# A relative-bias table that the host spreads over queries and near keys, loaded by one plain DMA

## The chip, the cores and the metric

The kernel runs on one core of a Trainium2 chip. The metric is the device time of one execution in microseconds (us). The kernel before took 1336.9 us as the median of three runs, which lay between 1336.58 and 1338.81 us. All data is float32; most large products split their operands into two float32r parts and take three passes over them.

## The reference

One encoder layer over 1024 tokens of 1024 features. A combined input projection feeds two head groups, their outputs are concatenated and projected, and a SwiGLU network with 2816 hidden features follows. Of it, only the attention group touches the changed table:

```
score = sum_h iw[h] * relu(iq[h] . ik)          # the indexer, 4 heads
idx   = top 256 keys of each query, chunk-causal
logits = q . k[idx] / 8 + rel_bias[t5_bucket(idx - qpos)]
p = softmax(logits);  out = p @ v[idx]
```

`rel_bias` has 32 rows (buckets) and 8 columns (heads). `t5_bucket` depends on the distance between key and query alone. For all keys 128 or more positions back it gives bucket 15. A softmax doesn't change when a constant is added to a row, so the kernel uses `rel_bias[bucket] - rel_bias[15]` and adds nothing for far keys.

## The kernel before

Tokens are taken in 8 blocks of 128. Stage 1 is the input projection of blocks 0 to 3 (`in_proj(0)`), with 11 chunks of weight columns, each multiplied with four blocks; then the same for blocks 4 to 7, the output projection and the feed-forward network of the first half, and the same of the second. In the trace the products of the projections are the matmuls that write tile `d`; each chunk's weights are loaded from DRAM on SP's DMA queue into `wraw`, and split into `whi` (ScalarE) and `wlo` (VectorE).

Everything else runs as background work between these products: jobs are Python generators in threads (`w` weights, `sel` index scores and top-k, `key`, `ret` retention, `att` attention, `bias`, `root` norms; lines 38 to 40). At build time, `tick` (line 874) is called after every group of large products. It lets a job issue its next step when a rough clock says that the step's data is there (plus 0.7 us) and that VectorE and ScalarE have at most 4 us of backlog (2 us for `bias`). `charge` (line 802) advances that clock; it takes a DMA as 2 us plus its bytes at 250 GB/s. So the order of instructions on each engine is fixed when the kernel is built, and each engine executes its own list in order.

`bias_tables` (line 230) is such a job. It is queued by `tables` (line 1099) after the first chunk. It loads `rel_bias` and a one-hot table of 32 x 384 on ScalarE's DMA queue, multiplies them (TensorE, tile `t`), copies the 8 x 384 result to `f` (VectorE, tile `rl`), and then on SP's queue writes `f` 128 times over to a DRAM scratch (`skew`, 8 x 128 x 384 floats):

```
nc.sync.dma_start(scr[:].rearrange("p h c -> h p c"), f[:, None, :].to_broadcast([8, 128, 384]))
```

The next step reads the scratch back on SP's queue with a row pitch one element short, so that each of 128 queries gets its own shifted window of 256 near keys (`bias`, 128 x 8 x 256), and masks a corner with a memset. `attention` (line 681) waits, at build time, until `self.bias` is set, and its first reduction of every head reads `bias` (line 735): directly for blocks 0 and 1, and through `mb` (line 715) from block 2 on. The logits go to the PSUM tile `l`, of which there is one buffer (line 720), so the next head's logits wait until VectorE has read the last one's.

On SP's queue stand, beside the weights, the loads of `x` for the row norms of blocks 4 to 7 (`x_stats`, line 370, tile `maA`); ScalarE squares them into `waste`.

Of the kernel before, what the change touches and what calls it, by code (L numbers as in the profile page):

```python
# [6 lines left out]
F32 = mybir.dt.float32  # L7
# [4 lines left out]
OP = mybir.AluOpType  # L12
AX = mybir.AxisListType
PSUM = bass.MemoryType.PSUM
DRAM = bass.MemoryType.DRAM
# [3 lines left out]
KT = 8  # L19
H = 8  # L20
DH = 64
TOPK = 256
# [5 lines left out]
NEG = -1.0e30  # L28
BIG = 3.0e38
SUB = 2                      # steps in which one load of weights is split  # L30
WARM = 11                    # products of zeros while the first operands are on their way
VALUES, PAIRS, GATES = 4, 4, 2          # tiles of the retention between projection and use

# The rough clock (us) that places background work: latencies between engines, the power on GpSimd.
# [3 lines left out]
# Threads of background work: most backlog (us) of VectorE or ScalarE, jobs at once, time from the end of a step to the next.  # L38
# [6 lines left out]
def host_constants():  # L45
    f = np.float32
    pos = np.arange(S, dtype=np.float64)
    inv = 10000.0 ** (-np.arange(32, dtype=np.float64) / 32)
    ang = (pos.astype(f)[:, None] * inv.astype(f)[None, :]).astype(np.float64)
    cos = np.cos(ang).astype(f).reshape(NB, 128, 32).transpose(1, 0, 2)  # L50
    sin = np.sin(ang).astype(f).reshape(NB, 128, 32).transpose(1, 0, 2)
    lg = np.log1p(-(2.0 ** (-5.0 - np.arange(H, dtype=np.float64))))
    dq = np.exp((pos + 1.0)[:, None] * lg[None, :])
    dk = np.exp(-(pos + 1.0)[:, None] * lg[None, :]) * DH ** -0.5
    dec = np.concatenate([dq, dk], axis=1).astype(f).reshape(NB, 128, 16).transpose(1, 0, 2)
    rel = np.arange(384) - 255
    n = np.abs(rel)
    nf = np.maximum(n, 1).astype(f)
    large = 8 + (np.log(nf / f(8)) / f(np.log(16.0)) * f(8)).astype(np.int32)
    bucket = np.where(rel > 0, 16, 0) + np.where(n < 8, n, np.minimum(large, 15))  # L60
    bkt = np.zeros((32, 384), f)
    bkt[bucket, np.arange(384)] = 1.0
    bkt[15, :] -= 1.0
    bits = np.tile((np.uint32(1) << np.arange(32, dtype=np.uint32))[None, :], (128, 1))
    eye = np.eye(128, dtype=f)
    return {
        "cos": np.ascontiguousarray(cos), "sin": np.ascontiguousarray(sin),
        "dec": np.ascontiguousarray(dec), "bkt": bkt, "bits": bits, "eye": eye,
        "causal": np.triu(np.ones((128, 128), f)),
    }  # L70


def layouts(host):
    """x with the features of a block of tokens on the partitions, the weights of its norm alike."""
    x = host["x"].reshape(NB, 128, KT, 128)
    return {"xt": np.ascontiguousarray(x.transpose(0, 3, 2, 1)).reshape(NB, 128, KT * 128),
            "n1": np.ascontiguousarray(host["norm1_w"].reshape(KT, 128).T)}


def extent(v):  # L80
    """The first and the last column that an access touches in its partition."""
    lo = v.offset % v.ap[0][0] if v.ap[0][0] else 0
    return lo, lo + sum(abs(st) * (n - 1) for st, n in v.ap[1:]) + 1


class Engine:
    """An engine whose instructions also advance a rough clock of it, by which background work is placed."""
# [28 lines left out]
class Layer:  # L116
    def __init__(self, tc, a, out, stack):
        self.tc, self.nc, self.a, self.out = tc, Engines(self, tc.nc), a, out
        self.clock = {"tensor": 0.0}
        self.busy = {"vector": [], "scalar": [], "gpsimd": []}  # L120
        self.issued_at, self.at, self.floor, self.issued = 0.0, 0.0, 0.0, 0
        self.written, self.touched, self.rings = {}, {}, {}
        self.x = a["x"][0]
        self.w_in, self.w_out = a["w_in"][0], a["w_out"][0]
        self.w_gate, self.w_up, self.w_down = a["w_gate"][0], a["w_up"][0], a["w_down"][0]
        pool = lambda n, **k: stack.enter_context(tc.tile_pool(name=n, **k))
        self.per = pool("per", bufs=1)
        self.dr = pool("dr", bufs=1, space=DRAM)

# [1 line left out]
    def new(self, pool, shape, dt, tag, bufs):  # L131
        """A tile; what is known of the time when its buffer comes free goes into the clocks."""
        t = pool.tile(shape, dt, tag=tag, name=tag, bufs=bufs)
        ring = self.rings.setdefault(tag, [])
        ring.append(t[:].tensor.name)
        if len(ring) > bufs:
            self.written[ring[-1]] = [(0, 1 << 30, self.touched.get(ring[-1 - bufs], 0.0), "")]
        return t
# [26 lines left out]
    def first_loads(self):  # L165
        """What the first product waits for, the array kept at work until then."""
# [37 lines left out]
    def roots(self):  # L204
        """The roots of the means' counts, in the weights of the norms."""
        nc = self.nc
        nc.vector.tensor_scalar(self.kw, self.kw, DH ** 0.5, None, op0=OP.mult)
        nc.vector.tensor_scalar(self.kvw, self.kvw, 128 ** 0.5, None, op0=OP.mult)
# [21 lines left out]
    def bias_tables(self):  # L230
        nc, a = self.nc, self.a
        rb = self.sb([32, 8], tag="rb")
        nc.scalar.dma_start(rb, a["rel_bias"])
        bkt = self.sb([128, 512], tag="rl", bufs=2)[:32, :384]
        nc.scalar.dma_start(bkt, a["bkt"])
        yield
        p = self.pt(384)
        nc.tensor.matmul(p[:8], rb, bkt, start=True, stop=True)
        f = self.sb([128, 512], tag="rl", bufs=2)[:8, :384]
        nc.vector.tensor_copy(f, p[:8])  # L240
        scr = self.dr.tile([128, 8, 384], F32, name="skew")
        nc.sync.dma_start(scr[:].rearrange("p h c -> h p c"), f[:, None, :].to_broadcast([8, 128, 384]))
        yield
        self.bias = self.sb([128, H, 256], tag="bias")
        full = scr[:]
        nc.sync.dma_start(self.bias, bass.AP(tensor=full.tensor, offset=full.offset + 127,
                                             ap=[[8 * 384 - 1, 128], [384, 8], [1, 256]]))
        nc.vector.memset(self.bias[0:64, :, 192:256], NEG)

# [1 line left out]
    def rsqrt(self, out, ssum, eps, more=None):  # L251
        """(ssum + more + eps) ** -0.5; the root of a mean's count goes into the weights that follow."""
# [22 lines left out]
    def pieces(self, loads, step, n, rows):  # L275
        """The tiles of one chunk of weights and the steps that fill them."""
# [6 lines left out]
        def fill():  # L283
            late = None
            for i, parts in enumerate(loads):
# [3 lines left out]
                tag, bufs = ("sc", 2) if first and i == 3 else ("wraw", 3)  # the scores come later  # L289
# [22 lines left out]
    def split_in(self, src, slot, g):  # L312
        """The half g, whose features are on the partitions already."""
# [44 lines left out]
    def x_block(self, b):  # L358
        """A block of tokens, weighed and split; its columns' root mean square is left to the products' ends."""
# [10 lines left out]
    def x_stats(self, b):  # L370
        """The root mean square of a block of tokens, a step before the factors that come of it."""
# [242 lines left out]
    def topk(self, bs):  # L614
        """Exact TOPK-th largest of every row, built bit by bit in the order of the float keys; the next candidate
        is the last one with its next bit flipped, and the last bit flipped back if that was too much.

        A pass sums sign(x - t), that is 2 * #(x > t) + #(x == t) - n, so the largest t that passes is the
        wanted value or its predecessor; one exact count settles which."""
# [153 lines left out]
    def heads_out(self, b, hp, pa):  # L773
        """The sums of the products with both parts of V, two heads above each other; the sum itself a step later."""
# [27 lines left out]
    def charge(self, name, op, args, kw):  # L802
        """Advance the clock (us) of an engine by one instruction on its operands."""
# [39 lines left out]
    def book(self, name, start, cost):  # L843
        """The first time from start on at which an engine has room for an instruction."""
# [20 lines left out]
    def step(self, th, job):  # L865
        """One step of a job; whether it issued anything."""
# [293 lines left out]
```

## Time and profile before

| | |
|---|---|
| median of 3 runs | 1336.9 us |
| the profiled execution, span from first to last instruction | 1335.8 us |
| TensorE busy | 1296.0 us, 97% of the span |
| VectorE busy | 887.2 us, 66% |
| ScalarE busy | 722.7 us, 54% |
| mean granted TensorE clock | 0.989 of full speed |
| share of the chain that ended last: TensorE / VectorE / ScalarE / DMA | 66% / 13% / 11% / 5% |

The chain that ended last is followed back from the last instruction, at each step to what released it; its DMA share of 5% contains 3% for a single transfer, `skew<-rl`. Line 96 is the helper that issues every instruction, so instructions are known by their tiles. "d<-whi,Thi" is a product of `whi` and `Thi` into `d`. SPq and ACTq are the instructions that issue DMAs from SP and ScalarE; q1 is the DMA queue of SP and q10 that of ScalarE. The busy time of TensorE is modelled and overlaps, so the number of products started in a stretch says more of its pace than its busy time.

### The profile page before, as it was taken

To read this page: it belongs to the slowest core of one execution; us is meant where nothing else is said; L and a number is where in the kernel's file an instruction comes from. 1 tells how busy PE (TensorE), PEld (TensorE's weight loads), DVE (VectorE), ACT (ScalarE), POOL (GpSimd) and SP (SyncE) were. 2 spreads that over 40 slices of the span, in tenths; PEclk is the share of its full clock that TensorE was granted. 3 is DMA by queue.
4 is the path that set the end of the run, shared out by engine and by line. 5 is a ranking of instruction groups with operands and counts; after the bars stand their busy time and mean duration, and the time that the engine had idled before them with its cause. 6 is when DMAs were issued, how large, how long until landed. Compare 5 with 4: busy or idle time off the path is not lost.

```text
span 1335.8 us, 21094 instructions
## 1 busy us (share of the span) xinstructions
PE 1296.0 (97%) x7621; PEld 1123.2 (84%) x7621; DVE 887.2 (66%) x2535; ACT 722.7 (54%) x1706; POOL 55.4 (4%) x68
## 2 busy tenths in 40 slices
PE   8969998999999899999999999999999999999998
PEld 7859998999999787888888878889988888888886
DVE  6649998888987877887877776645644343434343
ACT  7648977556695788478559834432532222222221
POOL 1300011010020000000000000000000000000000
PEclk9979999999999999999999999999999999999999
DMA  8552214221242222222222222326143333333331
GB/s 289 111 135 73 80 35 125 68 72 41 64 130 77 76 68 81 78 64 82 82 78 76 79 80 65 93 86 198 57 127 96 90 97 90 96 92 95 93 92 68
DMA packets 159665, 122.86 MB, mean 92 GB/s; under 512 B 8104, under 2 KB 139848, under 8 KB 159560
## 3 DMA queue, kind: packets, MB, share of 16 engines
q1 hardware_dynamic: 153816, 113.77, 29.7%
q10 hardware_dynamic: 5744, 7.74, 1.7%
q8 instruction: 60, 0.98, 0.3%
q14 instruction: 45, 0.37, 0.1%
HBM read 115.71 MB, written 5.77 MB: 91 GB/s over the span
## 4 chain that ended last, share of the span: by engine, by line
PE 66%; DVE 13%; ACT 11%; DMA 5%; issue 4%; POOL 1%; SPq 0%; ACTq 0%; POOLq 0%; DVEq 0%
PE d L96 56%; PE t L96 8%; ACT junk L96 6%; DVE wlo L96 3%; DMA skew<-rl 3%; DVE L L96 2%; PE l L96 2%; ACT whi L96 2%; ACT L L96 1%; ACT Thi L96 1%; DVE maA L96 1%; DVE tc L96 1%; DVE tr L96 1%; DMA wraw<-in_w_in_dram 1%; ACT ph L96 0%
## 5 line engine op out<-in xcount | busy, mean ns | idle before, releaser
L96 ACT ACTIVATE whi<-wraw 128x512 fp32r<-128x512 f32 (+1 forms) x388 | 220.8, 617 | 253.9 <-PE d L96 178.0
L96 PE MATMUL d<-whi,Thi 128*128 128x256 f32 (+1 forms) x960 | 281.9, 294 | 4.8 <-DVE zqk L96 1.9
L96 PE MATMUL d<-Thi,whi 128*128 128x512 f32 (+1 forms) x736 | 285.8, 389 | 0.2 <-ACT Thi L96 0.2
L96 PE MATMUL d<-Tlo,whi 128*128 128x512 f32 (+1 forms) x736 | 284.9, 387 | 0.4 <-DVE Tlo L96 0.4
L96 PE MATMUL d<-Thi,wlo 128*128 128x512 f32 (+1 forms) x736 | 284.5, 387 | 0.0
L96 PE MATMUL d<-wlo,Thi 128*128 128x256 f32 (+1 forms) x960 | 272.2, 284 | 2.0 <-DVE wlo L96 2.0
L96 PE MATMUL d<-whi,Tlo 128*128 128x256 f32 (+1 forms) x960 | 272.4, 284 | 0.0
L96 DVE TENSOR_TENSOR wlo<-wraw,whi 128x512 fp32r<-128x512 f32 (+1 forms) x390 | 251.8, 675 | 7.1 <-ACT whi L96 6.6
L96 PEld LDWEIGHTS d<-whi,Thi 128*128 128x128 f32 x960 | 182.2, 190 | 10.5 <-DVE zqk L96 2.3
L96 PEld LDWEIGHTS d<-wlo,Thi 128*128 128x128 f32 x960 | 182.3, 190 | 3.6 <-DVE wlo L96 2.8
L96 PEld LDWEIGHTS d<-whi,Tlo 128*128 128x128 f32 x960 | 182.0, 190 | 0.2 <-issue 0.2
L96 ACT ACTIVATE junk<-sc,tc 128x384 bf16<-128x384 f32 (+5 forms) x186 | 163.5, 879 | 32.7 <-DVE tc L96 32.0
L96 PEld LDWEIGHTS d<-Thi,wlo 128*128 128x128 f32 x736 | 139.3, 189 | 30.4
L96 PEld LDWEIGHTS d<-Tlo,whi 128*128 128x128 f32 x736 | 139.4, 189 | 28.4 <-DVE Tlo L96 0.7
L96 PEld LDWEIGHTS d<-Thi,whi 128*128 128x128 f32 x736 | 139.1, 189 | 28.6 <-ACT Thi L96 0.7
L96 PE MATMUL d<-whi,hh 128*128 128x512 f32 x352 | 140.1, 398 | 0.1
L96 PE MATMUL d<-wlo,hh 128*128 128x512 f32 x352 | 139.1, 396 | 0.0
L96 PE MATMUL d<-whi,hl 128*128 128x512 f32 x352 | 138.7, 396 | 0.0
L96 DVE TENSOR_TENSOR th<-th,d 128x512 f32<-128x512 f32 x44 | 30.1, 684 | 99.4 <-PE d L96 99.3
L96 PEld LDWEIGHTS d<-whi,hh 128*128 128x128 f32 x352 | 66.2, 188 | 16.3 <-DVE maA L96 0.6
L96 PEld LDWEIGHTS d<-whi,hl 128*128 128x128 f32 x352 | 66.2, 188 | 16.0
L96 PEld LDWEIGHTS d<-wlo,hh 128*128 128x128 f32 x352 | 66.2, 188 | 14.8
(306 smaller groups left out, 1731.0 us busy)
## 6 DMA issues: line engine op xcount, KB each, us to landing
wraw<-in_w_gate_dram SPq DMA_DIRECT2D x88, 256.0 KB, 3.1
wraw<-in_w_up_dram SPq DMA_DIRECT2D x88, 256.0 KB, 3.6
wraw<-in_w_down_dram SPq DMA_DIRECT2D x44, 512.0 KB, 3.8
wraw<-in_w_in_dram SPq DMA_DIRECT2D x24, 512.0 KB, 3.7
wraw<-in_w_in_dram SPq DMA_DIRECT2D x32, 256.0 KB, 3.5
wraw<-in_w_out_dram SPq DMA_DIRECT2D x16, 512.0 KB, 3.6
maA<-in_x_dram SPq DMA_DIRECT2D x20, 256.0 KB, 5.0
wraw<-in_w_in_dram SPq DMA_DIRECT2D x7, 292.0 KB, 3.9
```

What stands on the lines that cost most here:

```text
L96: return f(*args, **kw)
```

## The change

The host now builds a table `near` of 128 x 8 x 256 floats: `rel_bias` at the bucket of (key - query - 128) for each query of a block, head and near key. The device loads it with one DMA on ScalarE's queue, loads row 15 of `rel_bias` to all partitions with another, and subtracts it on VectorE in two instructions of four heads each, one per step of the job. The one-hot table, the product, the copy, the DRAM scratch and both DMAs on SP's queue are gone. Nothing else changes but comments and docstrings.

```diff
+def buckets():
+    f = np.float32
+    rel = np.arange(256)[None, :] - np.arange(128)[:, None] - 128
+    ...
 def layouts(host):
     x = host["x"].reshape(NB, 128, KT, 128)
+    near = np.ascontiguousarray(host["rel_bias"][buckets()].transpose(0, 2, 1))
     ...
     def bias_tables(self):
         nc, a = self.nc, self.a
-        rb = self.sb([32, 8], tag="rb")
-        nc.scalar.dma_start(rb, a["rel_bias"])
-        bkt = self.sb([128, 512], tag="rl", bufs=2)[:32, :384]
-        nc.scalar.dma_start(bkt, a["bkt"])
-        yield
-        p = self.pt(384)
-        nc.tensor.matmul(p[:8], rb, bkt, start=True, stop=True)
-        f = self.sb([128, 512], tag="rl", bufs=2)[:8, :384]
-        nc.vector.tensor_copy(f, p[:8])
-        scr = self.dr.tile([128, 8, 384], F32, name="skew")
-        nc.sync.dma_start(scr[:].rearrange("p h c -> h p c"), f[:, None, :].to_broadcast([8, 128, 384]))
-        yield
-        self.bias = self.sb([128, H, 256], tag="bias")
-        full = scr[:]
-        nc.sync.dma_start(self.bias, bass.AP(tensor=full.tensor, offset=full.offset + 127,
-                                             ap=[[8 * 384 - 1, 128], [384, 8], [1, 256]]))
-        nc.vector.memset(self.bias[0:64, :, 192:256], NEG)
+        far = self.sb([128, 8], tag="far")
+        nc.scalar.dma_start(far, a["rel_bias"][15:16, :].to_broadcast([128, 8]))
+        bias = self.sb([128, H, 256], tag="bias")
+        nc.scalar.dma_start(bias, a["near"])
+        yield
+        for h in (0, 4):
+            nc.vector.tensor_tensor(bias[:, h:h + 4], bias[:, h:h + 4], far[:, h:h + 4, None].to_broadcast([128, 4, 256]),
+                                    op=OP.subtract)
+            if h == 4:
+                nc.vector.memset(bias[0:64, :, 192:256], NEG)
+                self.bias = bias
+            yield
```

## Rows read from the trace of the kernel before

**Rows 1.** Chain that ended last, 16 to 90 us: start us, us, what.
```profile
37.06 4.27 DMA rl<-in_bkt_dram
42.30 0.56 DVE rl L96
42.88 33.61 DMA skew<-rl
```

**Rows 2.** TensorE in order of time: start us, us, instruction [idle before <-releaser].
```profile
41.46 0.80 PE L96 MATMUL t<-rl,rb 32*8 32x384 f32 x2 [0.90 <-DMA rl<-in_bkt_dram]
...
83.57 0.47 PE L96 MATMUL l<-kkhi,qT 128*128 128x128 f32 x1 [11.74 <-DVE nm L96]
```

**Rows 3.** SP's queue in order of time, 48 to 77 us.
```profile
48.33 9.10 SPq L96 DMA_DIRECT2D maA<-in_x_dram  x2
...
76.55 0.38 SPq L96 DMA_DIRECT2D bias<-skew  x1
```

**Rows 4.** DMA issues from 44 to 76 us: KB each, us to landing.
```profile
maA<-in_x_dram SPq DMA_DIRECT2D x2, 256.0 KB, 26.8
wraw<-in_w_in_dram SPq DMA_DIRECT2D x1, 256.0 KB, 21.2
```

**Rows 5.** ScalarE and VectorE in order of time, 77 to 84 us.
```profile
77.16 0.63 ACT L96 ACTIVATE waste<-maA 128x512 bf16<-128x512 f32 x1 [9.09 <-DMA maA<-in_x_dram]
...
83.34 0.63 ACT L96 ACTIVATE whi<-wraw 128x512 fp32r<-128x512 f32 x1 [4.69 <-DMA wraw<-in_w_in_dram]
...
82.52 0.48 DVE L96 MEMSET bias<- 64x512 f32 x1 [2.67 <-DMA bias<-skew]
```

**Rows 6.** Stretches: us, busy PE PEld DVE ACT POOL (instructions), PEclk, DMA share, GB/s.
```profile
60.00:68.00 8.00, 8.00 (x71) 8.00 (x71) 1.97 (x6) 1.74 (x4) 0.00 (x0) 1.00 0.53 65
78.00:80.00 2.00, 0.00 (x0) 0.00 (x0) 0.58 (x4) 0.64 (x2) 1.03 (x2) 0.50 0.98 310
84.00:92.00 8.00, 7.84 (x36) 7.12 (x35) 6.67 (x19) 6.69 (x19) 0.00 (x0) 0.52 0.64 167
92.00:100.00 8.00, 7.74 (x60) 6.92 (x59) 7.49 (x21) 6.04 (x24) 0.00 (x0) 1.00 0.18 49
```

**Rows 7.** VectorE groups by shape: count | busy us, mean ns | idle before.
```profile
L96 DVE TENSOR_TENSOR mb<-bias,sc 128x512 f32<-128x512 f32 x24 | 16.4, 682 | 0.1
L96 DVE SCALAR_TENSOR_TENSOR sc<-rl,iw,sc 128x512 f32<-128x512 f32 x18 | 13.4, 746 | 4.8 <-ACT rl L96 4.8
```

**Rows 8.** DMA: the read of the scratch, its KB and us to landing; queues from 24 to 28 us.
```profile
bias<-skew SPq DMA_DIRECT2D x1, 1024.0 KB, 5.8
...
q10 hardware_dynamic: 426, 0.58, 49.5%
q1 hardware_dynamic: 456, 0.46, 34.5%
```

**Rows 9.** ScalarE's issues of the two table loads, in order of time.
```profile
35.88 0.34 ACTq L96 DMA_DIRECT2D rb<-in_rel_bias_dram  x1
...
37.06 0.33 ACTq L96 DMA_DIRECT2D rl<-in_bkt_dram  x1
```

**Rows 10.** Longer stretches, same columns as the other table of stretches.
```profile
44.00:52.00 8.00, 7.42 (x62) 7.12 (x61) 6.31 (x21) 6.01 (x19) 5.04 (x6) 1.00 0.46 48
...
40.00:200.00 160.00, 144.77 (x1157) 137.28 (x1156) 125.00 (x511) 115.40 (x354) 20.03 (x21) 0.95 0.34 80
100.00:200.00 100.00, 98.41 (x818) 93.79 (x817) 91.86 (x413) 82.83 (x260) 9.01 (x8) 1.00 0.22 63
340.00:400.00 60.00, 59.69 (x503) 59.15 (x502) 52.37 (x184) 47.54 (x112) 10.52 (x10) 1.00 0.34 106
...
460.00:465.00 5.00, 2.35 (x12) 1.69 (x12) 4.90 (x14) 5.00 (x16) 0.00 (x0) 0.87 0.50 141
465.00:470.00 5.00, 5.00 (x24) 4.82 (x23) 2.86 (x9) 1.11 (x3) 0.00 (x0) 0.50 0.64 174
```

**Rows 11.** VectorE in order of time: the end of block 0's attention.
```profile
108.98 0.19 DVE L96 RECIPROCAL rec<-sums 128x8 f32<-128x8 f32 x1
```

More of the change, by code (lines that the diff above doesn't have):

```diff
@@ L14 @@
 PSUM = bass.MemoryType.PSUM
-DRAM = bass.MemoryType.DRAM
 S, D = 1024, 1024
@@ L55, in host_constants @@
     dec = np.concatenate([dq, dk], axis=1).astype(f).reshape(NB, 128, 16).transpose(1, 0, 2)
[L56 to L63, printed above, removed]
     bits = np.tile((np.uint32(1) << np.arange(32, dtype=np.uint32))[None, :], (128, 1))
@@ L67, in host_constants @@
         "cos": np.ascontiguousarray(cos), "sin": np.ascontiguousarray(sin),
-        "dec": np.ascontiguousarray(dec), "bkt": bkt, "bits": bits, "eye": eye,
+        "dec": np.ascontiguousarray(dec), "bits": bits, "eye": eye,
         "causal": np.triu(np.ones((128, 128), f)),
     }
+def buckets():
+    f = np.float32
+    rel = np.arange(256)[None, :] - np.arange(128)[:, None] - 128
+    n = np.abs(rel)
+    nf = np.maximum(n, 1).astype(f)
+    large = 8 + (np.log(nf / f(8)) / f(np.log(16.0)) * f(8)).astype(np.int32)
+    return np.where(rel > 0, 16, 0) + np.where(n < 8, n, np.minimum(large, 15))
 def layouts(host):
     x = host["x"].reshape(NB, 128, KT, 128)
+    near = np.ascontiguousarray(host["rel_bias"][buckets()].transpose(0, 2, 1))
     return {"xt": np.ascontiguousarray(x.transpose(0, 3, 2, 1)).reshape(NB, 128, KT * 128),
-            "n1": np.ascontiguousarray(host["norm1_w"].reshape(KT, 128).T)}
+            "n1": np.ascontiguousarray(host["norm1_w"].reshape(KT, 128).T), "near": near}
 def extent(v):
@@ L127, in __init__ @@
         self.per = pool("per", bufs=1)
-        self.dr = pool("dr", bufs=1, space=DRAM)
     def new(self, pool, shape, dt, tag, bufs):
```

## The prediction

> **What bounds the kernel now.** The page comes first: TensorE is busy 97% of the span, so the end moves only where TensorE waits or where its clock is low. The chain of waits comes second, because it names what stands there. Its one long piece that isn't a product is the write of the DRAM scratch: 33.61 us from 42.88 us on, ahead of it the load of the one-hot table (4.27 us) and the copy of its product (0.56 us) [rows 1]. The third view is TensorE in order of time: in that stretch it stands still for 11.74 us, up to 83.57 us, at the logits of a second attention head; they need the PSUM buffer that VectorE empties, which is to read the bias [rows 2]. SP's list shows why the bias is so late: the read of the scratch could be issued only at 76.55 us, after the write had landed [rows 3], and VectorE, which executes its list in order, stood until 82.52 us at the memset that waits for that read [rows 5].
>
> The write also holds up what is behind it. Two loads for the row norms took 9.10 us to be issued [rows 3] and 26.8 us to land, a load of weights 21.2 us [rows 4]; a read of 1024 KB, four times as much as one of these, landed in 5.8 us [rows 8]. ScalarE waited for those norms until 77.16 us and for weights until 83.34 us [rows 5]. So bias, norms and weights are late together, all behind one write; with it, all three waits go. Last, the table of stretches: by 78 us the granted clock is 0.50, its lower level of 1.2 GHz, after TensorE had been idle, and from 84 to 92 us it is 0.52 while TensorE works [rows 6].
>
> **The change part by part.** The profiled execution spans 1335.8 us; the median is 1336.9, so what lies around the span and the difference between runs make 1.1 us, which I add at the end.
>
> *The stall.* Removed with the write and the read: 11.74 us of idle TensorE [rows 2]. I take all of it, 11.7. Next in line in that stretch would be the weights, but they were late only behind the write.
>
> *The clock.* Between 84 and 92 us TensorE started 36 products, between 60 and 68 us, at full clock and with nothing late, 71 [rows 6]: 8 x (1 - 36/71) = 3.9 us lost. The clock alone gives the same: 8 x (1 - 0.52) = 3.8 us. If the attention's own chain paces this stretch as it does from 92 to 100 us at full clock (60 products), the loss is 8 x (60 - 36)/71 = 2.7 us; I take 3.9, since the count and the clock agree. The 8 x (1 - 60/71) = 1.2 us of the stretch from 92 to 100 us I don't count: attention is in the queue there whatever the bias does.
>
> *The product.* TensorE waits 0.90 us for the one-hot table and works 0.80 us in two passes [rows 2]: 1.7 us gone. At least the 0.8 goes; something else that is late there could take the wait.
>
> *The new loads.* They are issued on ScalarE's queue where the old two were, at 35.9 to 37.1 us [rows 9], the big one right behind the small one, some 36.3 us. The table has as many bytes as the read of the scratch, which landed in 5.8 us [rows 8]: 42.1 us. Weights and norms are on SP's queue at the same time. From 24 to 28 us, when both queues were full, ScalarE's moved 0.58 MB, 0.145 MB/us [rows 8]; by that, 1.05 MB take 7.2 us and, with some 2 us for its start and its end (an estimate: 5.8 us less the 4.0 that 1.05 MB take at both queues' 0.26 MB/us), the table lands at 45.5. When does VectorE come to it? The old product was reached at 41.46 - 0.90 = 40.6 us, 4.7 us after its load; the rough clock had put 2.2 + 0.7 us between them. It puts 6.2 + 0.7 us between the new load and the first subtraction, 4.0 more: 44.6 us. So VectorE waits from 0 to 0.9 us, in a place where it is idle anyway (6.31 of 8 us busy from 44 to 52 us [rows 10]).
>
> Here the Trainium skill speaks against a second queue (DMA: Bandwidth & Descriptors, "Queues, rings and completion order"): each DMA engine takes turns between the queues that have work for it, so a load from ScalarE's queue takes its share from SP's. The trace agrees: both queues were served side by side from 24 to 28 us [rows 8]. By the rule the table lands at 45.5 us, by the lone transfer at 42.1; what a much later landing does is the second rival.
>
> *VectorE.* Two subtractions of 128 x 1024. A two-operand instruction on 128 x 512 takes 0.68 us, the slowest kind of that shape 0.75 [rows 7]; twice the columns give 1.36 to 1.5 us, less the fixed part, so 1.3 us each. The copy of 0.56 us [rows 1] goes, the memset stays: 2 x 1.3 - 0.56 = 2.0 us more. VectorE has 8 - 6.31 = 1.7 us free from 44 to 52 us [rows 10], which hides most: I charge 0.5; without cover it is 2.0. What stands behind the subtractions on VectorE are splits of weights and the index scores; whoever waits for those is TensorE.
>
> *What is late next.* VectorE's work doesn't go, it moves into less time. From 40 to 200 us it is busy 125.0 of 160 us [rows 10]; afterwards (125.0 + 2.0)/(160 - 17.3) = 89%, about the 92% of 100 to 200 us, where TensorE starts 818 products in 100 us against 71 in 8 [rows 6, 10]. The mix differs (attention has products of other sizes), so 1 - 8.18/8.88 = 8% is an upper bound of what a loaded VectorE costs; over the 40 us from 44 to 84 us, which had no attention so far, that is 3.2 us. The lower bound is 0. I take 2.0, nearer the upper end, since the row that it rests on is the same work.
>
> *Sum.* 1335.8 - 11.7 - 3.9 - 1.7 + 0.5 + 2.0 = 1321.0 us of span, and 1.1: **1322 us**. TensorE is the bound before and after; top-k and the attention of later blocks start earlier by the same amount, so I let the gain stand to the end.
>
> **Rivals.**
> *The new order also removes a later stall.* From 460 to 470 us TensorE idles 2.65 of 5 us and then has the clock at 0.87 and 0.50 [rows 10]: 2.65 + 0.13 x 2.35 + 2.5 = 5.5 us. Attention of the second half meets the output projection there. The order is planned anew, so this may dissolve: 1322 - 5.5 = 1316.5. For it: the bias comes some 4 us earlier in the rough clock's plan. Against it: the work there is that of other blocks, and a new stall of this size is as possible (1327.5).
>
> *The table lands late.* If the load of 1 MB among weights takes 15 us instead of 6 to 9, VectorE stands in its list from 44.6 to 51.3 us: 6.7 us, after which TensorE has nothing to do and the clock falls for a while (half of the next 4 us, 2.0 in sum): 1322 + 8.7 = 1331. For it: loads took over 20 us in this kernel [rows 4]. Against: those were behind the write, and the same bytes landed in 5.8 us [rows 8].
>
> *It comes out slower.* The attention of blocks 0 to 3 must be issued by the last chunk of the second input projection, where `drain("ret", "att")` (line 1112) issues what is left with nothing beside it. The top-k of blocks 2 and 3 comes earlier now and has precedence over attention (line 39); if a whole block's attention slips behind the drain, it costs what block 0's took when little ran beside it, from 82.52 to 108.98 us [rows 5, 11], 26.5 us: 1348. It decides from 15/26.5 = 56% of a block on. Against it: from 340 to 400 us, where the drain is, TensorE is busy 59.69 of 60 us [rows 10], so nothing is left over now, and the bias comes sooner, not later.
>
> *No change.* Something else would hold TensorE at 72 to 84 us: weights at 83.34 us, norms at 77.16 us [rows 5]. If these are late for a reason of their own, the stall stays, 1336. Against it: what was late, a load of weights and two of norms [rows 4], was issued while the write was in flight [rows 1, 3], and the read after it wasn't late [rows 8].
>
> **How the numbers follow.** Forecast 0.73, later stall gone too 0.10, table late 0.10, slower 0.04, no change 0.03. A measurement tells about 0.2%, 2.7 us, from no change. Faster: 0.73 + 0.10 + 0.10, less 0.01 for a table later still: 0.92; within 0.2%: 0.04; slower: 0.04. The forecast's own bounds: 1322 - 1.2 - 2.5 = 1318 (the stretch after the slow clock gained, no new cost), and 1322 + 1.2 + 1.5 + 1.2 + 0.9 = 1327 (less from the clock, subtractions uncovered, full load cost, wait at the product replaced). Adding most of the first two rivals, 1314 to 1331.
>
> **What would show it.** Right: no scratch in the DMA list; no idle of TensorE over 2 us between 40 and 100 us and a granted clock of 1.00 there; loads for norms landing in 3 to 9 us; attention of block 0 done by about 80 us instead of 109. Wrong: VectorE waiting for the table over 2 us; TensorE waiting longer for VectorE after 100 us than before; new stretches at half clock.

## The result, and the profile after

The changed kernel takes 1321.86 us (median of four runs, 1320.95 to 1324.31) against 1337.04 us of the kernel before beside it: a ratio of 0.9885, 95% interval 0.9871 to 0.9899. It is 15.2 us faster; 1322 us was forecast. The sum came out, but two of its steps did not: the table costs more than forecast, and a later stall went that I had left in place. That the two nearly cancel is luck.

First the granted clock in 40 slices, from the page of the changed kernel. No slice (33 us each) is below 9 now; before, the third was 7.

```profile
PEclk9999999999999999999999999999999999999999
```

Next the stretches of the changed kernel in the columns of [rows 6], ahead of them the DMA issues from 36 to 50 us as in [rows 4, 8].

```profile
bias<-in_near_dram ACTq DMA_DIRECT2D x1, 1024.0 KB, 7.9
maA<-in_x_dram SPq DMA_DIRECT2D x4, 256.0 KB, 6.6
wraw<-in_w_in_dram SPq DMA_DIRECT2D x2, 256.0 KB, 7.6
```

```profile
44.00:48.00 4.00, 0.25 (x3) 0.04 (x1) 2.68 (x6) 0.92 (x4) 1.33 (x2) 1.00 0.29 107
48.00:52.00 4.00, 3.07 (x14) 3.10 (x15) 3.62 (x13) 2.50 (x8) 2.42 (x3) 0.63 0.25 66
...
84.00:92.00 8.00, 7.89 (x66) 7.18 (x65) 5.79 (x30) 5.88 (x23) 0.00 (x0) 1.00 0.23 64
```

Loads of 256 KB land in 6.6 to 7.6 us where they took 21.2 and 26.8 [rows 4]. From 84 to 92 us 66 products start at full clock; before it was 36 at 0.52 [rows 6]. But from 44 to 48 us TensorE hardly works, and from 48 to 52 us its clock is 0.63 on average. The reason stands in VectorE's list and in the chain that ended last (start, us, what) of the changed kernel; the last two fences are ScalarE and TensorE in order of time.

```profile
40.36 0.41 DVE L99 TENSOR_REDUCE ssq<-t 128x4 f32<-128x256 f32 x1
45.24 1.23 DVE L99 TENSOR_TENSOR bias<-bias,far 128x1024 f32<-128x1024 f32 x1 [4.47 <-DMA bias<-in_near_dram]
```

```profile
37.26 7.89 DMA bias<-in_near_dram
45.24 1.23 DVE bias L99
...
46.70 0.35 DVE kklo L99
```

```profile
47.09 0.28 ACT L99 ACTIVATE ikT<-t 128x128 fp32r<-128x128 f32 x1 [4.86 <-DVE kklo L99]
```

```profile
43.97 0.28 PE L99 MATMUL d<-wlo,Thi 128*128 128x256 f32 x1
48.93 0.57 PE L99 MATMUL t<-ikT,iqT 128*128 128x384 f32 x1 [4.68 <-ACT ct L99]
```

VectorE comes to the first subtraction at 40.8 us and stands 4.47 us until the table has landed. The key work of the next blocks (`kklo`) is behind it in the list. ScalarE waits 4.86 us for `kklo`, the tile `ct` stands behind that in ScalarE's list, and TensorE, whose next work needs it, pauses for 4.68 us.

**Where the time came from** is read best along the 6144 products of the projections (those that write `d`, without the 11 products of zeros at the start). Every kernel executes them in nearly the same order: at most 39 of them stand at another place. "Lead" at the n-th product is its start in the kernel before less its start in the other kernel, less the same difference at product 96, the end of the first chunk. What lies ahead of product 96 is left out because the change doesn't act there, and two profiles of one kernel differ by up to 2.6 us there. (The expectations of e1, e2 and e5 below count from the start of the span instead; the changed kernel's 9.0 in them is the 10.1 here.) I worked the leads out from all products of each trace. Product 1056 is the end of the first input projection (205 us before), 2400 and 2800 enclose the stretch from 430 to 532 us, 6144 is the last.

| lead in us at product | 1056 | 2400 | 2800 | 6144 | time, us |
|---|---|---|---|---|---|
| the changed kernel | 10.1 | 9.6 | 16.4 | 16.3 | 1321.86 |
| e8, the same again | 9.5 | 9.1 | 15.9 | 15.9 | 1321.67 |
| e1, no table | 16.8 | 16.0 | 22.9 | 24.8 | 1313.38 |
| e2, loads earlier | 11.3 | 12.2 | 21.4 | 18.9 | 1319.05 |
| e3, write from 128 partitions | 13.8 | 9.2 | 16.4 | 16.9 | 1320.78 |
| e4, write on GpSimd's queue | -25.5 | -33.2 | -25.9 | -25.5 | 1363.68 |
| e5, subtractions held | 16.1 | 11.0 | 18.4 | 22.1 | 1317.65 |
| e9, the same again | 15.9 | 11.1 | 18.4 | 22.1 | 1316.34 |
| e6, order alone | 1.2 | 1.1 | 6.8 | 5.5 | 1333.36 |
| e7, write from 16 partitions | 14.5 | 14.3 | 15.0 | 14.9 | 1323.92 |
| e10, held and order | 16.0 | 12.2 | 20.4 | 22.4 | 1318.36 |

The times of e3, e4 and e7 are single runs, the others medians of four to seven; each lead is from one profile. Two profiles of one kernel agree within 0.6 us in every column (the changed kernel with e8, e5 with e9). So the change gains 10.1 us in the first 205 us and another 6.8 between products 2400 and 2800, around the stall at 460 us. A lead between two products that lie close together misleads: background products of TensorE can move out of such a stretch into a neighbouring one. Between products 2520 and 2616 alone the lead grows by 10.1 us, but there the kernel before executes 53 other products and the changed one 33. From 2400 to 2800 it is 156 and 151, so most of the 6.8 us is the stall.

### The profile page after: what moved, and what is told of

The parts are those of the page before. It is cut to its first block, busy times and chain, and to the rows that moved or that the text cites. A ratio compares the mean times of both kernels' runs of the same rounds, so it can differ in the third digit from the quotient of the medians.

```text
span 1320.6 us, 21083 instructions
## 1 busy us (share of the span) xinstructions
PE 1290.5 (98%) x7619; PEld 1119.0 (85%) x7619; DVE 889.4 (67%) x2536; ACT 723.3 (55%) x1706; POOL 57.5 (4%) x68
## 4 chain that ended last, share of the span: by engine, by line
PE 74%; DVE 12%; ACT 8%; issue 2%; DMA 2%; POOL 2%; ACTq 0%; SPq 0%; DVEq 0%; POOLq 0%
PE d L99 64%; PE t L99 8%; ACT junk L99 3%; DVE wlo L99 2%; PE l L99 2%; DVE L L99 1%; ACT whi L99 1%; ACT Thi L99 1%; DMA bias<-in_near_dram 1%; ACT waste L99 1%; DVE zqk L99 0%; DVE plo L99 0%; DMA mb__101<-in_xt_dram 0%; DVE junk L99 0%; DVE tr L99 0%
## 5 line engine op out<-in xcount | busy, mean ns | idle before, releaser
L99 PEld LDWEIGHTS d<-whi,hh 128*128 128x128 f32 x352 | 66.1, 188 | 16.8 <-DVE mb__5825 L99 1.4
```

Of the source, the lines that this page charges most:

```text
L99: return f(*args, **kw)
```

## The experiments

**e1, the table left out.** Both loads and both subtractions go; the bias is zeros, so the relative bias is missing from the result.

```diff
-        nc.scalar.dma_start(far, a["rel_bias"][15:16, :].to_broadcast([128, 8]))
-        nc.scalar.dma_start(bias, a["near"])
+        self.at = self.clock["tensor"] + 6.2
 ...
-            nc.vector.tensor_tensor(bias[:, h:h + 4], ...)
+            nc.vector.memset(bias[:, h:h + 4], 0.0)
```

> The changed kernel without the table: its two loads and the two subtractions are left out, and the bias is a memset of zeros (this leaves the relative bias out of the result). My theory: the change's own price is VectorE's wait for the table (4.5 us) and TensorE's pause and slow clock behind it, some 7 us in all, so at the last product of the first input projection this kernel is 15 to 17 us ahead of the kernel before, where the changed one is 9.0 ahead; the end is 1314 to 1317 us. Rival: VectorE's load sets the pace of that stage anyway, and the lead there stays 9 to 10 us; the end is 1321 to 1323 us.

1313.38 us, ratio 0.9822 (0.9806 to 0.9839). The lead at product 1056 is 16.8 against 10.1 us: the table with its loads and subtractions costs 6.7 us there, and the rest of VectorE's load isn't what holds that stage. The end came 0.6 us below the range expected.

**e2, the loads earlier.** They are issued in `constants2`, ahead of the bit masks (37.3 to 31.9 us).

```diff
 ...
+        nc.scalar.dma_start(self.far, a["rel_bias"][15:16, :].to_broadcast([128, 8]))
 ...
+        nc.scalar.dma_start(self.near, a["near"])
         nc.scalar.dma_start(self.bits, a["bits"])
 ...
```

> The changed kernel with the two loads issued six to eight us earlier, ahead of the load of the bit masks. My theory: the table lands before VectorE reaches the first subtraction, its wait falls from 4.5 to under 1 us, the pause of TensorE from 44 to 49 us goes, the lead at the end of the first input projection is 13 to 16 us instead of 9.0; 1314 to 1318 us. Rival: the 1 MB now delays weights that TensorE needs sooner, a pause of 3 to 5 us comes up between 30 and 40 us instead, and the time stays within 1320 to 1324 us.

1319.05 us (0.9849 to 0.9879), lead 11.3: the pause moved, as the rival had it, though it's a little shorter and the time a little under the rival's range. VectorE waits 1.2 us for the table, and TensorE now pauses at 35 us. From e2, TensorE and a stretch:

```profile
37.96 0.49 PE L99 MATMUL t<-wukv,ct 128*128 128x128 f32 x2 [2.62 <-ACT ct L99]
```

```profile
36.00:40.00 4.00, 2.04 (x11) 1.97 (x12) 2.70 (x7) 3.71 (x14) 0.93 (x1) 0.86 0.98 358
```

The DMA engines are full (0.98), ScalarE waits 1.5 us for a load of `x` just before, and TensorE waits for ScalarE. That the 1 MB pushes back what is needed there at once fits this; no run shows it by itself.

**e3, the write from 128 partitions.** The kernel before, its product made for 16 copies of the 8 heads, the scratch written in 8 DMAs.

```diff
+        rb16 = ...                              # rb 16 times over, copied on VectorE
-        nc.tensor.matmul(p[:8], rb, bkt, start=True, stop=True)
+        nc.tensor.matmul(p, rb16, bkt, start=True, stop=True)
 ...
-        nc.sync.dma_start(scr[:].rearrange("p h c -> h p c"), f[:, None, :].to_broadcast([8, 128, 384]))
+        for i in range(8):
+            nc.sync.dma_start(scr[16 * i:16 * i + 16].rearrange("r h c -> (r h) c"), f)
```

> The kernel before, with the one-hot product made for 128 rows (16 copies of the 8 heads) and the scratch written from 128 partitions in 8 DMAs of the same total bytes, the readback unchanged. Theory: the write from 8 partitions was slow because it used few DMA engines (the DMA share stood at 0.46); from 128 partitions it takes 4 to 10 us instead of 33.6, loads behind it land in under 10 us, the 11.7 us stall shrinks under 3 us; 1320 to 1327 us. Rival: writing 1.5 MB to DRAM is slow in itself, the write still takes over 25 us and the time stays at 1335 to 1338 us.

1320.78 us in one run. The DMA issues of e3, from 43 to 52 us:

```profile
skew<-rl SPq DMA_DIRECT2D x8, 192.0 KB, 2.2
```

The eight writes land 2.2 us after their issue (median), and they are issued between 43.4 and 46.7 us. With the scratch, the product and the readback all still there, the kernel is as fast as the changed one. So most of what the change gains doesn't come from the detour over DRAM being gone, but from one badly shaped write being gone. Its order of instructions is new too (the lead falls to 9.2 and rises again by 7.2), so the end alone doesn't show this; the 13.8 us at product 1056 do, and e7 with the old order.

**e4, the write and the read on GpSimd's queue**, the kernel before otherwise.

```diff
-        nc.sync.dma_start(scr[:]...
+        nc.gpsimd.dma_start(scr[:]...
-        nc.sync.dma_start(self.bias, ...
+        nc.gpsimd.dma_start(self.bias, ...
```

> The kernel before, with the scratch's write and its read on GpSimd's queue instead of SP's. Theory: the bias is as late as before (read landed at 78 to 90 us), but weights and norms aren't behind the write any more and land in 4 to 9 us; TensorE still waits for the bias at the second head's logits wherever the order of instructions puts it before that, so over half of the gain is missing: 1328 to 1337 us. Rival: weights and norms were what held TensorE, and the time is 1320 to 1326 us although the bias comes as late as before.

1363.68 us in one run, outside both expectations. Its DMA issues from 44 to 78 us, and what waited longest from 40 to 125 us (engine, awaited, us in total, times, longest):

```profile
skew<-rl POOLq DMA_DIRECT2D x1, 1536.0 KB, 34.9
wraw<-in_w_in_dram SPq DMA_DIRECT2D x6, 256.0 KB, 23.7
```

```profile
POOL rc L96 <- DVE rq L96: 62.9, 1, 62.9
ACT whi L96 <- DMA wraw<-in_w_in_dram: 21.9, 1, 21.9
```

The weights are late on their own queue too (23.7 us against 21.2 [rows 4]): my expectation that they'd land in 4 to 9 us failed. ScalarE stood 21.9 us for them, and the readback, which stands behind other work in GpSimd's list, went out only at 114.6 us. So loads needn't be behind the write in one queue to be late; being in flight beside it is enough. Since bias and weights both stayed late, this run can't tell which of them held TensorE. The Trainium skill says what fits (DMA: Bandwidth & Descriptors, "Queues, rings and completion order"): each DMA engine takes turns between queues, a packet at a time. By that rule a load waits for packets of the write between its own; the single packets weren't looked at here.

**e5, the subtractions held.** The changed kernel; its loads stay, but the subtracted row gets zero times a norm factor of block 5 added, which is known only later.

```diff
+        while 5 not in self.scaled:
+            yield
+        zero = self.small(1, "zero", bufs=1)
+        nc.vector.tensor_scalar(zero, self.rsh[:, 5:6], 0.0, None, op0=OP.mult)
+        nc.vector.tensor_scalar(far, far, zero, None, op0=OP.add)
         for h in (0, 4):
```

> The changed kernel with the loads where they are, and the subtractions made to depend on the norm factors of block 5 (by adding zero times such a factor to the subtracted row), so that they stand some 10 instructions later in VectorE's list. Theory: the price of the table is that VectorE reaches the subtraction at 40.8 us, before the table has landed at 45.1, and stands there; now its wait for the table is under 0.5 us, TensorE's pause at 44 to 49 us goes, the lead over the kernel before at the end of the first input projection is 13 to 16 us instead of 9.0, and the time is 1314 to 1318 us. Rival: the price is the 1 MB itself, beside weights and norms on the DMA engines; a pause of TensorE of over 2 us stays between 40 and 60 us, the lead stays at 9 to 11 us and the time at 1320 to 1323 us.

1317.65 us (0.9834 to 0.9867), lead 16.1 against 10.1 us at product 1056. The stretches of e9, the same kernel once more:

```profile
44.00:48.00 4.00, 4.00 (x35) 4.00 (x35) 3.50 (x12) 1.83 (x5) 1.74 (x3) 1.00 0.47 170
48.00:52.00 4.00, 3.34 (x28) 3.14 (x28) 3.37 (x11) 3.87 (x12) 2.32 (x4) 1.00 0.00 0
```

Between 44 and 52 us TensorE has some 60 products where the changed kernel has 17, and the clock stays at 1.00. VectorE's wait for the table is gone; the same 1 MB is loaded, issued at 36.9 us against 37.3. So of the 6.7 us that the table costs there, 6.0 are the place of the subtraction, not the bytes: a pause of 4.68 us and 4 x (1 - 0.63) = 1.5 us of clock behind it. These 6.0 us aren't simply carried to the end, though. The held kernel loses 5.1 us by product 2400, where its lead over the changed kernel is only 1.4, and gets 3.7 after product 2800; of its 5.8 us at the end, much is thus a matter of the later order, which wasn't taken apart.

**e6, order alone.** The kernel before, with a longer pause (1.2 us instead of 0.7) between steps of attention on the rough clock from the output projection on.

```diff
             self.lmax = 1024
+            self.threads["att"].gate = 1.2
```

> The kernel before, in which only the pause between steps of attention is raised from 0.7 to 1.2 us on the rough clock from the output projection on; nothing of the first half of the span changes. Theory: the 7 to 9 us that all variants gained around product 2600 (455 to 470 us) hang on the order of instructions there and not on the lead; here too most of it is gained, with the stall of 11.7 us at 72 us as before: 1328 to 1334 us. Rival: the stall there comes from work that the lead brings forward, and without a lead it stays: 1335 to 1338 us.

1333.36 us (0.9958 to 0.998). The stretches of e6; the stall at 72 us is there, that of 460 us is not:

```profile
72.00:84.00 12.00, 1.13 (x10) 0.92 (x8) 1.31 (x6) 1.50 (x5) 1.53 (x2) 0.70 0.77 197
...
460.00:465.00 5.00, 4.16 (x34) 4.16 (x35) 4.73 (x16) 3.51 (x11) 0.00 (x0) 1.00 0.71 203
465.00:470.00 5.00, 5.00 (x32) 4.41 (x31) 4.52 (x14) 2.64 (x7) 0.00 (x0) 1.00 0.36 105
```

The lead grows by 5.7 us between products 2400 and 2800, with 1.1 us before; 5.5 us are left at the end. The counts of other products in that stretch are the same as before, 156 and 156, so this is the price of the later stall.

**e7, the write from 16 partitions**, each head twice, the scratch laid out by heads; the kernel before otherwise.

```diff
+        rb2 = ...                               # rb twice, copied on VectorE; product and copy for 16 rows
 ...
-        scr = self.dr.tile([128, 8, 384], F32, name="skew")
-        nc.sync.dma_start(scr[:].rearrange("p h c -> h p c"), f[:, None, :].to_broadcast([8, 128, 384]))
+        scr = self.dr.tile([8, 128, 384], F32, name="skew")
+        nc.sync.dma_start(scr[:].rearrange("h (s q) c -> (h s) q c", s=2), f[:, None, :].to_broadcast([16, 64, 384]))
 ...
```

> The kernel before, with the scratch laid out by heads and written from 16 partitions (each head twice) in one DMA instead of from 8, the same bytes in the same rows of 1536 bytes. Theory: the pace of the write is a fixed rate for each partition that it reads (1536 KB from 8 partitions in 33.6 us is 5.8 KB/us each); from 16 partitions it takes 16 to 18 us; the stall at 72 us shrinks to 0 to 4 us; 1320 to 1330 us. Rival: the stride of the rows in the scratch set the pace; now it takes under 8 us as from 128 partitions.

1323.92 us in one run. First the DMA issue of the write in e7, then stretches of e7: that of the write, and two in the later stall:

```profile
skew<-rl SPq DMA_DIRECT2D x1, 1536.0 KB, 18.0
```

```profile
46.00:58.00 12.00, 11.42 (x94) 11.11 (x94) 8.92 (x29) 10.67 (x29) 6.44 (x9) 1.00 0.92 97
...
445.00:450.00 5.00, 3.27 (x18) 2.53 (x17) 4.17 (x10) 4.94 (x14) 0.00 (x0) 0.87 0.14 40
450.00:455.00 5.00, 4.38 (x18) 3.71 (x18) 4.28 (x15) 2.36 (x8) 0.00 (x0) 0.50 0.95 266
```

Twice the partitions, half the time (33.6 to 18.0 us). TensorE, ScalarE and VectorE execute the lists of before here, but for one added copy on VectorE and the one-hot product itself. So this run shows the effect of the slow write by itself, the late bias and what is late behind it: 14.5 us at product 1056, 14.9 at the end. The later stall is still there, with the same 0.87 and 0.50 of the clock as in [rows 10], only 15 us earlier. A lead without a new order keeps the stall (e7), a new order without a lead removes it (e6).

**e8, e9, e10.** The changed kernel and e5 once more, and e5 with the edit of e6.

> The changed kernel once more, beside the next two on the same chip: 1320 to 1324 us, and the lead over the kernel before between the end of the first chunk and the end of the first input projection 9 to 11 us, as in its first profile. If the lead there moves by more than 2 us from profile to profile, no reading of leads under that is worth anything.

> The kernel with the held subtractions once more: theory, it stays 3 to 6 us under the changed kernel on the same chip (1316 to 1319 us), since the pause behind VectorE's wait is gone in every execution. Rival: its 1317.65 us was a difference of chip and moment, and both lie within 2 us of each other.

> The held subtractions, and attention's pause on the rough clock raised to 1.2 us from the output projection on. Theory: both kernels on their own avoid the stall around 460 us already, so the second edit has nothing left to gain there and moves the end only as any new order does, by at most 4 us either way: 1314 to 1322 us. Rival: the gains add up, 4 us under the held kernel: 1312 to 1314 us.

1321.67 us (0.9867 to 0.99), 1316.34 us (0.983 to 0.986), 1318.36 us (0.9846 to 0.9875). The held kernel is 5.3 us under the changed one on one chip and its interval lies wholly below; it beats both kernels. e10 is no better than e9, as the first theory had it: its lead at the end, 22.4 against 22.1, is the same, and its median is 2.0 us longer.

## Why the prediction was right, step by step

**The stall and the clock: right.** I took 11.7 + 3.9 us, less 2.0 for the work that is now denser: 13.6. e7, which removes only the lateness of the bias and of the loads behind the write, leads by 14.5 us at the end of that stage. The price for density was probably nearer its lower bound: with no table at all (e1) the lead is 16.8 of the 17.3 us that stall, clock and product promised, so by that sum 0.5 us is left for it, not 2.0. That is as small as the 0.6 us by which two profiles differ.

**The product: not shown, but it fits.** e5 and e1 lead e7 by 1.6 and 2.3 us at product 1056, with the product gone; 1.7 was forecast. No run took it away alone, and these kernels differ in more than that.

**The new loads: the step that failed.** The landing was right (45.1 us measured; 42.1 to 45.5 forecast). The time at which VectorE comes to it was not: 40.8 us, not 44.6, so VectorE waits 4.47 us instead of 0 to 0.9, and TensorE pauses 4.68 us in a place that I had called idle anyway. With the slow clock behind it, that is the 6.0 us between e5 and the changed kernel. My mistake was to read the order of VectorE's list off the rough clock. That clock orders the calls; the lists that the engines execute can have another order. The subtraction comes 3.5 us after the issue of the big load (37.26 us), just as the old product came 3.5 us after that of the one-hot table [rows 2, 9]: the 4.0 us more on the rough clock don't show. And e1 shows a reordering outright. Its memsets of the bias are called by a job that is queued after the first chunk (product 96 starts at 24.4 us before), yet they ran from 2.1 us on:

```profile
L99 DVE MEMSET bias<- x3: 485/912/912, 2.1 to 4.3; 128x1024 f32 x2, 64x512 f32 x1
```

That the same reordering moved the subtraction is likely, not shown; that it stands too early in VectorE's list is shown by e5. In its effect this is the second rival (a wait of 6.7 us and 8.7 us in all by its terms, 4.47 and some 6 measured), though not in its cause: the table wasn't later than forecast, the instruction was earlier.

**The later stall: wrong, and it made the number right.** I let the gain stand to the end and gave the end of the later stall one chance in ten. It did go: the lead grew by 6.8 us between products 2400 and 2800, 5.7 in e6 with the order alone. The price that I had worked out for it, 5.5 us, was about right. The sum by measured leads is 10.1 - 0.5 + 6.8 - 0.1 = 16.3 us; mine at product 1056 was 17.3 - 2.5 = 14.8, and nothing after it (the 15.2 us by the medians and the 16.3 differ by what lies before product 96 in these profiles, 1.1 us). The two errors, 4.7 us too much in stage 1 and 6.2 too little afterwards, nearly cancel. That the time came out at 1322 us is luck: with the error in stage 1 alone it would have been near 1327 (an estimate, 1322 + 4.7), the upper end of the forecast's own bounds. That the stall of before hangs on the order of instructions is shown from both sides (e6, e7); why just this order has it, beyond VectorE at 4.90 and ScalarE at 5.00 of 5 us [rows 10], stays open.

**The signs to look for.** Scratch gone, loads for norms at 6.6 us: as forecast. "No idle of TensorE over 2 us between 40 and 100 us" failed at 44 us, and the clock of 1.00 failed from 48 to 52 us (0.63). Two of the signs of being wrong came up too, VectorE's wait of over 2 us for the table and a new stretch at the lower clock. Attention of block 0 wasn't done by 80 us but at 103.9, only 5 us sooner than before [rows 11]: it now runs beside other work instead of after a stall. The slower rival didn't appear in this kernel: from 340 to 400 us TensorE is busy 59.22 of 60 us.

## What to carry to other kernels

A DMA's price isn't its bytes alone: look at its shape (here from how many partitions, and in how many DMAs), and at who lands late while it runs; reshaping one write (e3, e7) gave about as much as this change did by removing the whole detour. When a load is hidden behind other work, find the place of its first consumer in that engine's own instruction list, since an in-order engine that arrives four us early stops everything behind it. And a new build order can move distant stalls by over half as much as the edit itself (6.8 and 10.1 us here): compare kernels along a sequence that both execute, not by the end alone, and count what else stands between the two places that you compare.

## What the runs showed of the hardware

A write of 1536 KB out of SBUF took 33.6 us from 8 partitions and 18.0 us from 16, 5.7 and 5.3 KB/us for each partition; from 128 the eight parts landed 2.2 us after issue (median). While 8 partitions were read, the DMA share was 0.46 [rows 10], with 16 it was 0.92 at only 97 GB/s: busy DMA engines, slow bytes. The Trainium skill (DMA: Bandwidth & Descriptors, "Why a DMA increments its semaphore by 16 and not by 1") says that a DMA uses the largest number of engines, up to 16, that divides the slowest dimension of both its sides. The shares for 8 and 16 agree (0.46 and 0.92, with 8 and 16 of 16 engines). By the number of engines alone the gain would end at 16, and the runs show more: e3's write, 16 engines by the same rule, takes some 5.5 us from the first issue to the last landing (an estimate, 46.7 + 2.2 - 43.4) against e7's 18.0. Whether a partition's read, the repeated source row or the number of rows per DMA sets that pace wasn't taken apart; e3 and e7 differ in all three.
